# First chunks of the value projection: SP's loads in program order, ScalarE ahead of VectorE on each bank of x, weights cast a pair ahead

## The chip, the cores and the metric

One core of a Trainium2 chip runs the whole kernel. TensorE multiplies, VectorE (DVE) and ScalarE (ACT) do elementwise work, GpSimd (POOL) a little of it, and SyncE (SP) issues nearly all DMAs. The metric is the device time of one execution in microseconds (us); it was 2045.33 us in the median of three runs (2045.03 to 2045.54).

## What is computed

A residual block for 512 tokens of width 2048, in float32: RMSNorm, one projection to queries, keys and values of 16 heads (8 of stick-breaking attention, 8 of forgetting attention) and 8 gates, the two attentions, an output projection, an MLP with squared ReLU, and a last RMSNorm.

```
h = rmsnorm(x, g_attn[l])
proj = jnp.einsum('bsd,de->bse', h, w_in[l])
...
x = x + jnp.einsum('bse,ed->bsd', mixed, w_out[l])
h2 = rmsnorm(x, g_mlp[l])
u = jax.nn.relu(jnp.einsum('bsd,df->bsf', h2, w_up[l]))
x = x + jnp.einsum('bsf,fd->bsd', u * u, w_down[l])
return rmsnorm(x, g_final)
```

The change lies in the first 50 us or so: x is loaded and transposed, and the values of the first two heads and the gates are projected while that goes on.

## The kernel before

**Precision.** A float32 operand is split into a high part (rounded to the type of TensorE's fast float32 mode) and a low part, the operand less its high part. A product is three matmuls: high by high, high by low, low by high (mm3, L75). So for each weight tile ScalarE casts the high part (Piece.cast, L166) and VectorE subtracts it (Piece.low, L170).

**Chunks, pairs, banks.** The 2048 columns of x are 16 chunks of 128. Chunk k and chunk k + 8 are pair k, and the order is 0, 8, 1, 9, ..., 7, 15 (seq, L264). A chunk goes through these steps, each a function of its own:
- turn_x (L230): four TensorE transposes bring 512 tokens of the chunk into one bank of PSUM (tr). The pool has two such banks, so the transposes of a chunk need the bank of the chunk but one before it, read out by everybody.
- x_high (L235): ScalarE scales the bank by g_attn and writes the high part, hH.
- x_low (L238): VectorE reads the bank again, scales it, subtracts hH and writes hL.
- x_more (L241, chunks 0 to 7): ScalarE writes the scaled chunk once more, in two halves, into x1 (x11 and x21).
- x_sum (L244, chunks 8 to 15): VectorE writes f5, the right half of the tokens of this chunk plus x21, and x12, the left half.
- first_values (L259): 12 matmuls, six for each half of the tokens, 128x264 each, into the banks vy and vz.

x1, x12 and f5 are the sources of sums that the later products use (sums_of_x, L330). Reads of one bank by ScalarE and by VectorE are kept apart by semaphores, in the order in which the program issues them.

**Weights.** Chunks 0 and 8 have a piece of weights each, 128x264; pairs 1 to 7 have one of 128x528 for both chunks. Raw pieces (wraw) share three buffers, and each is free again when its low part is formed. The split pieces (wh, wl) have three buffers too.

**The order of the work** is written by hand. Plan.at(t, f) (L148) notes a function with a due time, and Plan.run issues all of them sorted by that time. manual_schedule (L184) keeps TensorE, ScalarE and VectorE in just that order; each of them works strictly in order. SP is not in that list in the kernel before: its DMAs may be put in another order by the scheduler, which works from an estimate of times. Due times count from a notional start: chunk number n in seq is due at 6.5 + 1.93 n (mm_at, L266), and TV (L313) is the end of the last. In the trace SP issued x's first half of columns (xa: chunks 0 to 3 and 8 to 11), pieces 0 and 8 and the weights of pair 1, then xb (chunks 4 to 7 and 12 to 15, two loads of 1024 KB), and then the weights of pairs 2 to 7 mixed with four loads of q.

**What follows.** The values of the next heads come from seven products per group on quadrants of 1024 rows and 384 columns of the weights (product, L390; quadrants q "21", "11", "12", "22", each of four loads of 384 KB by load_quadrant, L304). Quadrant 21 of group 1 has a room of its own. Quadrants 11, 12 and 22 take the room of xa and xb, so their loads (open_quads, L380) wait until x has been squared: square_x (L249), eight ScalarE instructions of 1024 elements that sum the squares of x for its RMSNorm, four on xa and four on xb. The casts of q stand among the squares of xb on ScalarE.

Of the kernel before, what the change touches and what calls it, by code (L numbers as in the profile page):

```python
# [11 lines left out]
ALU = mybir.AluOpType  # L12
PSUM = bass.MemoryType.PSUM

P = 128
# [4 lines left out]
NH = 8  # L20
# [16 lines left out]
def block_kernel(ctx, tc, x, g_attn, w_in, b_f, g_out_sb, g_out_fox, w_out, g_mlp, w_up, w_down, g_final, y):  # L37
    nc = tc.nc
    pe, act, dve, pool, sp = nc.tensor, nc.scalar, nc.vector, nc.gpsimd, nc.sync
# [65 lines left out]
    g_in = cp.tile([P, KC], F32, name="g_in")  # L105
    g_rest = cp.tile([P, KC + 2 * NH], F32, name="g_rest")
    g_up, g_sb, g_fx = g_rest[:, :KC], g_rest[:, KC:KC + NH], g_rest[:, KC + NH:]
    bf = cp.tile([P, NH], F32, name="bf")
# [30 lines left out]
    K8 = KC // 2  # L139
# [43 lines left out]

    manual = tc.manual_schedule(engines={pe.engine, act.engine, dve.engine})  # L184
    manual.__enter__()

    first_piece = q_piece(0, 0, 0)
    with ExitStack() as stage:
# [4 lines left out]
        HALVES = slice(0, 4), slice(4, 8)  # L193

        x1 = vf.tile([P, 2, K8, 2 * P], F32, tag="e0", name="x1")
        x11, x21 = x1[:, 0], x1[:, 1]
# [16 lines left out]
        plan = Plan()  # L213
# [14 lines left out]
        turned = {}  # L228
# [12 lines left out]
        def x_more(k):  # L241
            act.mul(x1[:, :, k, :], turned[k].rearrange("p (s n) -> p s n", s=2), g_in[:, k:k + 1])

        def x_sum(k):  # L244
            g, a = g_in[:, k:k + 1], k - K8
            dve.scalar_tensor_tensor(f5[:, a, :], turned[k][:, 2 * P:], g, x21[:, a, :], op0=ALU.mult, op1=ALU.add)
            dve.tensor_scalar(x12[:, a, :], turned[k][:, :2 * P], g, None, op0=ALU.mult)

# [16 lines left out]
        t0, step = 6.5, 1.93  # L265
        mm_at = {j: t0 + step * n for n, j in enumerate(seq)}  # L266
        LOADS = {0: 1, 1: 1, 2: 2, 4: 4}
        pieces = {}
# [8 lines left out]
        for i, (f, *args) in enumerate(begin):  # L277
            plan.at(-50 + i, f, *args)
        for j in seq:
            k, t = j % K8, mm_at[j]  # L280
            plan.at(t - 2.95 if j else -1.0, turn_x, j)
            plan.at(t - 2.2, x_high, j)
            plan.at(t - 1.45, x_low, j)
            if j < K8:
                plan.at(t - 1.5, x_more, j)
            else:
                plan.at(t - 0.7, x_sum, j)
            w, i = pieces[j]
            if k == 0:
                plan.at(t - 2.1, w.cast)  # L290
                plan.at(t - 1.3, w.low)
            elif j < K8:
                if k > 3:
                    plan.at(t - 13, w.load)
                plan.at(t - 3.2, w.cast)
                plan.at(t - 2.6, w.low)
            for half in range(2):
                plan.at(t + 0.74 * half, first_values, j, w, i, half)
        plan.at(-60, columns, g_in, g_rows, KC)
        for t in range(TB):  # L300
            plan.at(mm_at[4 + t] - 0.8, square_x, 0, t)
        quads = {1: {}, 2: {}}
# [7 lines left out]

        plan.at(mm_at[6], load_quadrant, 1, "21", 0)

# [3 lines left out]
        def load_rows():  # L316
            i = 0
            for r in (g[0].rearrange("(h p) -> h p", p=P) for g in (g_mlp, g_out_sb, g_out_fox)):
                act.dma_start(rows_[i:i + r.shape[0], :], r)
                i += r.shape[0]  # L320
            act.dma_start(bf, b_f.to_broadcast([P, NH]))

# [3 lines left out]

        plan.at(mm_at[3] - 0.8, load_rows)
        plan.at(TV + 0.6, take_rows)
# [4 lines left out]

        plan.at(mm_at[5] - 0.7, sums_of_x, 7, HALVES[0])
        plan.at(mm_at[6] - 0.7, sums_of_x, 6, HALVES[0])
        plan.at(TV + 0.9, sums_of_x, 7, HALVES[1])
# [178 lines left out]
        first_piece.plan(plan, TV + 13 * TP, TV + 14 * TP - 3.5, TV + 14 * TP - 1.5)  # L515
        plan.run()

    acc_cms = [tc.tile_pool(name=f"acc{c}", bufs=2, space=PSUM, reuse_waits="tile") for c in "ab"]
# [1332 lines left out]
```

## Time and profile before

| | |
|---|---|
| median of three runs | 2045.33 us (2045.03 to 2045.54) |
| the profiled execution | 2044.84 us |
| its span in the trace | 2043.1 us |
| HBM read / written | 313.62 MB / 96.49 MB |
| DMA issued through the hardware queues | 408.02 MB, 60.1% of 16 engines' span |

A line of the timeline reads: start in us, duration in us, engine, line of the kernel, operation, output<-inputs, shape, count, and in brackets how long the engine was idle before it and what ended that. PE is TensorE's matmul, PEld its weight load, SPq the issue of DMAs by SP. Consecutive instructions of an engine overlap by some 0.1 us at their ends. A line of the stretches reads: from and to, length, then for each engine its busy time and number of instructions, the clock granted to TensorE, the busy share of the DMA engines, and what they moved. A line of the groups reads: line, engine, operation, tiles and shapes, count, then busy time in all, mean of one in ns, and idle time before them. A line of the chain of waits reads: start, duration, what the end of the kernel hung on at that time. In the trace, hH of chunk n is x_high's output, tr the bank, x without a letter x1 or x12, f is f5.

### The profile page before, as it was taken

The numbers are of one execution on the slowest core, as the hardware profiler recorded it, in microseconds if no ns is written. First come the engines' busy times: TensorE is split into PE (matmuls) and PEld (weight loads), VectorE is DVE, ScalarE is ACT, GpSimd is POOL, SyncE is SP. The second block draws the span as 40 slices with busy tenths as digits, with TensorE's granted clock in tenths as the row PEclk, the third lists the DMA queues.
The fourth block names the chain that finished last, engine by engine and source line by source line (L and its number), as shares of the span: only waits on it lengthen the run. The fifth ranks groups of instructions, "written<-read, shape, count | busy, mean of one in ns | idle before, by whom it ended". The sixth has DMA issues, their size and how long they took to land.

```text
span 2043.1 us, 27164 instructions
## 1 busy us (share of the span) xinstructions
PE 2019.1 (99%) x10410; PEld 1744.4 (85%) x10410; DVE 1735.9 (85%) x1966; ACT 1129.8 (55%) x1618; POOL 64.8 (3%) x73
## 2 busy tenths in 40 slices
PE   8999999999999999999999999999999999999998
PEld 7898888888888888988888888888888888888887
DVE  5975777888867678899999999998798898888896
ACT  6543444455654566667677677676644444444344
POOL 0000011100000000000000000000000000000004
PEclk9999999999999999999999999999999999999999
DMA  5426666665547882656666667667685664674642
GB/s 188 152 94 214 196 206 201 194 218 181 181 134 273 279 277 90 220 173 194 213 193 213 197 197 221 189 206 258 227 293 211 223 253 174 235 249 179 223 163 83
DMA packets 269634, 411.88 MB, mean 202 GB/s; under 512 B 10248, under 2 KB 165432, under 8 KB 262976
## 3 DMA queue, kind: packets, MB, share of 16 engines
q1 hardware_dynamic: 268544, 408.02, 60.1%
q10 hardware_dynamic: 960, 2.13, 0.3%
q8 instruction: 82, 1.34, 0.3%
q14 instruction: 48, 0.39, 0.1%
HBM read 313.62 MB, written 96.49 MB: 201 GB/s over the span
## 4 chain that ended last, share of the span: by engine, by line
PE 92%; DVE 4%; DMA 2%; ACT 1%; issue 1%; SPq 0%; POOL 0%; ACTq 0%; DVEq 0%; POOLq 0%
PE psa L1088 10%; PE accd L78 8%; PE accd L76 8%; PE accd L77 8%; PE accq L76 5%; PE accq L78 5%; PE accq L77 5%; PE psa L1086 5%; PE psc L1088 5%; PE psc L1086 3%; PE psb L1088 3%; PE m L76 1%; PE m L77 1%; PE m L78 1%; PE psb L1086 1%; PE accoa L77 1%
## 5 line engine op out<-in xcount | busy, mean ns | idle before, releaser
L1663 ACT CAST wh<-wd 128x1024 fp32r<-128x1024 f32 x126 | 124.9, 999 | 166.7 <-PE accd L78 57.6
L1553 DVE TENSOR_TENSOR wl<-wu,wh 128x1024 fp32r<-128x1024 f32 x157 | 191.4, 1220 | 15.0 <-ACT wh L1547 14.9
L76 PE MATMUL accq<-hH,wh 128*128 128x512 f32 x512 | 201.7, 394 | 0.0
L78 PE MATMUL accq<-hH,wl 128*128 128x512 f32 x512 | 199.7, 390 | 0.0
L77 PE MATMUL accq<-hL,wh 128*128 128x512 f32 x512 | 199.6, 390 | 0.0
L1547 ACT CAST wh<-wu 128x1024 fp32r<-128x1024 f32 x157 | 166.4, 1060 | 47.5 <-PE psc L1088 20.8
L1088 PE MATMUL psa<-f,wh 128*128 128x512 f32 x728 | 181.1, 391 | 0.0
L77 PE MATMUL accd<-wl,uf 128*128 128x512 f32 x436 | 169.6, 389 | 0.0
L78 PE MATMUL accd<-wh,uf 128*128 128x512 f32 x436 | 169.6, 389 | 0.0
L76 PE MATMUL accd<-wh,uf 128*128 128x512 f32 x436 | 169.4, 389 | 0.0
L1088 PEld LDWEIGHTS psa<-f,wh 128*128 128x128 f32 x728 | 133.7, 188 | 25.8
L1670 DVE TENSOR_TENSOR wl<-wd,wh 128x1024 fp32r<-128x1024 f32 x126 | 144.0, 1152 | 13.2 <-ACT wh L1663 13.2
L1437 DVE TENSOR_TENSOR m<-m,accd 128x1024 f32<-128x1024 f32 x84 | 102.2, 1217 | 47.1 <-PE accd L78 47.1
L1663 ACT CAST wx<-wd 128x1024 fp32r<-128x1024 f32 (+1 forms) x82 | 80.8, 995 | 109.2 <-PE accd L78 43.1
L168 ACT CAST wh<-wraw 128x1024 fp32r<-128x1024 f32 (+2 forms) x77 | 76.7, 998 | 72.6 <-PE accq L77 59.7
L78 PEld LDWEIGHTS accq<-hH,wl 128*128 128x128 f32 x512 | 96.1, 188 | 20.3
L77 PEld LDWEIGHTS accq<-hL,wh 128*128 128x128 f32 x512 | 96.2, 188 | 18.6
L76 PEld LDWEIGHTS accq<-hH,wh 128*128 128x128 f32 x512 | 96.3, 188 | 18.5
L76 PE MATMUL accd<-wx,uf 128*128 128x512 f32 x284 | 110.5, 389 | 0.0
L77 PE MATMUL accd<-wx,uf 128*128 128x512 f32 x284 | 110.5, 389 | 0.0
L78 PE MATMUL accd<-wx,uf 128*128 128x512 f32 x284 | 110.5, 389 | 0.0
L1086 PEld LDWEIGHTS psa<-f,wl 128*128 128x128 f32 x728 | 97.0, 191 | 6.0 <-ACT l L1119 0.6
(418 smaller groups left out, 5110.5 us busy)
## 6 DMA issues: line engine op xcount, KB each, us to landing
wu<-in_w_up_dram SPq DMA_DIRECT2D x60, 1024.0 KB, 6.5
ufd<-st SPq DMA_DIRECT2D x98, 512.0 KB, 3.7
wd<-in_w_down_dram SPq DMA_DIRECT2D x48, 1024.0 KB, 8.4
uf<-ufd SPq DMA_DIRECT2D x42, 1024.0 KB, 6.9
wraw<-in_w_in_dram SPq DMA_DIRECT2D x68, 512.0 KB, 4.2
wo<-wsums SPq DMA_DIRECT2D x28, 512.0 KB, 4.7
q<-in_w_in_dram SPq DMA_DIRECT2D x32, 384.0 KB, 5.4
wd<-in_w_down_dram SPq DMA_DIRECT2D x16, 768.0 KB, 6.1
```

What stands on the lines that cost most here:

```text
L76: pe.matmul(out, sh, mh, start=first, stop=False, skip_group_check=True)
L77: pe.matmul(out, sh, ml, start=False, stop=False, skip_group_check=True)
L78: return pe.matmul(out, sl, mh, start=False, stop=last, skip_group_check=True)
L168: act.copy(self.hi, self.source())
L1086: ins = pe.matmul(ps[:, 2 * P:], lo[:, a, :], f_parts(p, a)[0], start=False, stop=last, skip_group_check=True)
L1088: ins = pe.matmul(ps, hi[:, a, :], f_both(p, a), start=a == PAIRS[0] and p in (1, 5), stop=last, skip_group_check=True)
L1437: dve.tensor_tensor(M[p][:, :, db, :], M[p][:, :, db, :], ps, op=ALU.add)
L1547: act.copy(rooms[k][0], srcs[k])
L1553: lows[0] = dve.tensor_tensor(lo, srcs.pop(k), hi.bitcast(F32), op=ALU.subtract)
L1663: act.copy(rooms[k + 3][0], srcs[k + 3])
L1670: dve.tensor_tensor(rooms[k + 2][1], srcs.pop(k + 2), rooms[k + 2][0].bitcast(F32), op=ALU.subtract)
```

## The change

SP is put under the hand-written order until the value products end (an exit and re-entry of manual_schedule then takes it out again), so DMAs are issued in the order of the plan. x_more moves from ScalarE to VectorE and comes behind x_low there. The half x12 moves from VectorE to ScalarE (x_right, new) and comes ahead of x_low. The due times are rewritten for each pair: on ScalarE x_high of k, the cast for pair k + 1, x_high of k + 8, x_right; on VectorE x_low of k, x_more, the low weights of pair k + 1, x_low of k + 8, x_sum. For the first pair, the transposes of chunk 8 stand between the two halves of chunk 0's matmuls. Squares and sums of x are due later by 1.6 and 2.7, the first quadrant's load is due with chunk 5 rather than chunk 6, and load_rows issues its four small loads from SP.

```diff
@@ -181,7 +181,7 @@
         c0 = (o0 if h >= NH else 0) + h % NH * P + which * WSB
         return Piece(w_in[half * K8 * P:(half + 1) * K8 * P, c0:c0 + P].rearrange("(a p) c -> p a c", p=P), K8, P)
 
-    manual = tc.manual_schedule(engines={pe.engine, act.engine, dve.engine})
+    manual = tc.manual_schedule(engines={pe.engine, act.engine, dve.engine, sp.engine})
     manual.__enter__()
 
     first_piece = q_piece(0, 0, 0)
@@ -239,12 +239,13 @@
             dve.scalar_tensor_tensor(hL[k], turned[k], g_in[:, k:k + 1], hH[k].bitcast(F32), op0=ALU.mult, op1=ALU.subtract)
 
         def x_more(k):
-            act.mul(x1[:, :, k, :], turned[k].rearrange("p (s n) -> p s n", s=2), g_in[:, k:k + 1])
+            dve.tensor_scalar(x1[:, :, k, :], turned[k].rearrange("p (s n) -> p s n", s=2), g_in[:, k:k + 1], None, op0=ALU.mult)
+
+        def x_right(k):
+            act.mul(x12[:, k - K8, :], turned[k][:, :2 * P], g_in[:, k:k + 1])
 
         def x_sum(k):
-            g, a = g_in[:, k:k + 1], k - K8
-            dve.scalar_tensor_tensor(f5[:, a, :], turned[k][:, 2 * P:], g, x21[:, a, :], op0=ALU.mult, op1=ALU.add)
-            dve.tensor_scalar(x12[:, a, :], turned[k][:, :2 * P], g, None, op0=ALU.mult)
+            dve.scalar_tensor_tensor(f5[:, k - K8, :], turned[k][:, 2 * P:], g_in[:, k:k + 1], x21[:, k - K8, :], op0=ALU.mult, op1=ALU.add)
 
         def square_x(half, t):
             x_ = xt[half][:, :, t, :]
@@ -264,7 +265,6 @@
         seq = [j for k in range(K8) for j in (k, k + K8)]
         t0, step = 6.5, 1.93
         mm_at = {j: t0 + step * n for n, j in enumerate(seq)}
-        LOADS = {0: 1, 1: 1, 2: 2, 4: 4}
         pieces = {}
         for j in (0, K8):
             pieces[j] = Piece(w_rows[0][:, j // K8:j // K8 + 1, c0:c0 + m], 1, m), 0
@@ -276,29 +276,28 @@
                  (load_x, 4, 4), (load_x, 12, 4)]
         for i, (f, *args) in enumerate(begin):
             plan.at(-50 + i, f, *args)
-        for j in seq:
-            k, t = j % K8, mm_at[j]
-            plan.at(t - 2.95 if j else -1.0, turn_x, j)
-            plan.at(t - 2.2, x_high, j)
-            plan.at(t - 1.45, x_low, j)
-            if j < K8:
-                plan.at(t - 1.5, x_more, j)
+        for k in range(K8):
+            t, j = mm_at[k], k + K8
+            for jj, dt in ((k, 0.0), (j, step)):
+                for half in range(2):
+                    plan.at(t + dt + 0.74 * half, first_values, jj, *pieces[jj], half)
+            w = pieces[k][0]
+            if k == 0:
+                w8 = pieces[8][0]
+                jobs = [(-5.0, turn_x, k), (-4.0, x_high, k), (-3.9, w.cast), (-3.5, x_low, k), (-3.4, w.low), (-3.3, x_more, k),
+                        (0.1, turn_x, j), (0.2, x_high, j), (0.3, w8.cast), (0.35, x_right, j), (0.4, x_low, j), (0.5, w8.low), (0.6, x_sum, j)]
             else:
-                plan.at(t - 0.7, x_sum, j)
-            w, i = pieces[j]
-            if k == 0:
-                plan.at(t - 2.1, w.cast)
-                plan.at(t - 1.3, w.low)
-            elif j < K8:
+                dt = mm_at[k - 1] - t
+                jobs = [(-2.95, turn_x, k), (-2.2, x_high, k), (-1.5, x_low, k), (-0.75, x_more, k),
+                        (-1.02, turn_x, j), (-0.3, x_high, j), (0.4, x_right, j), (0.85, x_low, j), (1.6, x_sum, j),
+                        (dt + (1.2 if k == 1 else -1.5), w.cast), (dt + (1.3 if k == 1 else -0.05), w.low)]
                 if k > 3:
-                    plan.at(t - 13, w.load)
-                plan.at(t - 3.2, w.cast)
-                plan.at(t - 2.6, w.low)
-            for half in range(2):
-                plan.at(t + 0.74 * half, first_values, j, w, i, half)
+                    jobs.append((-14.0, w.load))
+            for dt, f, *args in jobs:
+                plan.at(t + dt, f, *args)
         plan.at(-60, columns, g_in, g_rows, KC)
         for t in range(TB):
-            plan.at(mm_at[4 + t] - 0.8, square_x, 0, t)
+            plan.at(mm_at[4 + t] + 0.8, square_x, 0, t)
         quads = {1: {}, 2: {}}
 
         def load_quadrant(group, name, i):
@@ -308,7 +307,7 @@
             for a in range(0, K8, 2):
                 sp.dma_start(t_[:, a:a + 2], vrows[s][:, a:a + 2, c0:c0 + NV])
 
-        plan.at(mm_at[6], load_quadrant, 1, "21", 0)
+        plan.at(mm_at[5], load_quadrant, 1, "21", 0)
 
         TV = mm_at[KC - 1] + step - 0.2
         rows_ = xr.tile([KC + 2 * NH, P], F32, name="rows")
@@ -316,23 +315,23 @@
         def load_rows():
             i = 0
             for r in (g[0].rearrange("(h p) -> h p", p=P) for g in (g_mlp, g_out_sb, g_out_fox)):
-                act.dma_start(rows_[i:i + r.shape[0], :], r)
+                sp.dma_start(rows_[i:i + r.shape[0], :], r)
                 i += r.shape[0]
-            act.dma_start(bf, b_f.to_broadcast([P, NH]))
+            sp.dma_start(bf, b_f.to_broadcast([P, NH]))
 
         def take_rows():
             columns(g_rest, rows_, KC + 2 * NH)
             dve.tensor_scalar(g_rest[:, KC:], g_rest[:, KC:], -0.5 / P, None, op0=ALU.mult)
 
-        plan.at(mm_at[3] - 0.8, load_rows)
+        plan.at(mm_at[5] + 0.5, load_rows)
         plan.at(TV + 0.6, take_rows)
 
         def sums_of_x(p, a):
             out, u, v = {7: (x21, x11, x21), 6: (x11, f5, x11)}[p]
             dve.tensor_tensor(out[:, a], u[:, a], v[:, a], op=ALU.subtract)
 
-        plan.at(mm_at[5] - 0.7, sums_of_x, 7, HALVES[0])
-        plan.at(mm_at[6] - 0.7, sums_of_x, 6, HALVES[0])
+        plan.at(mm_at[5] + 2.0, sums_of_x, 7, HALVES[0])
+        plan.at(mm_at[6] + 2.0, sums_of_x, 6, HALVES[0])
         plan.at(TV + 0.9, sums_of_x, 7, HALVES[1])
         for t in range(TB):
             plan.at(TV - 2.4 + (0, 1.8, 3.6, 5.6)[t], square_x, 1, t)
@@ -514,6 +513,10 @@
                 plan.at(t + 7 * TP - 1.0, load_quadrant, 2, "22", 3)
         first_piece.plan(plan, TV + 13 * TP, TV + 14 * TP - 3.5, TV + 14 * TP - 1.5)
         plan.run()
+
+    manual.__exit__(None, None, None)
+    manual = tc.manual_schedule(engines={pe.engine, act.engine, dve.engine})
+    manual.__enter__()
 
     acc_cms = [tc.tile_pool(name=f"acc{c}", bufs=2, space=PSUM, reuse_waits="tile") for c in "ab"]
     accs = [cm.__enter__() for cm in acc_cms]
```

## The prediction

> **What bounds the kernel now.** I read the page first (span, busy shares, chain of waits), then stretches of the first 170 us, then the timeline where TensorE falls behind.
>
> ```profile
> span 2043.1 us, 27164 instructions
> PE 2019.1 (99%) x10410; PEld 1744.4 (85%) x10410; DVE 1735.9 (85%) x1966; ACT 1129.8 (55%) x1618; POOL 64.8 (3%) x73
> PE 92%; DVE 4%; DMA 2%; ACT 1%; issue 1%; SPq 0%; POOL 0%; ACTq 0%; DVEq 0%; POOLq 0%
> ```
>
> TensorE sets the end. All its idle time is 2043.1 - 2019.1 = 24 us, so a change that leaves the matmuls alone, as this one does, can win only from that and from time at a lower clock.
>
> ```profile
> core 0: us, PE busy (x) PEld busy (x) DVE busy (x) ACT busy (x) POOL busy (x), PEclk, DMA share, GB/s
> 7.27:17.64 10.37, 10.35 (x66) 10.09 (x64) 5.01 (x10) 3.58 (x6) 0.00 (x0) 1.00 1.07 396
> 17.64:21.24 3.60, 0.00 (x1) 0.01 (x1) 0.61 (x1) 1.27 (x3) 0.00 (x0) 1.00 1.07 394
> 27.73:47.14 19.41, 19.39 (x155) 18.45 (x154) 15.96 (x27) 16.47 (x29) 0.00 (x0) 1.00 0.14 35
> 60.00:100.00 40.00, 37.98 (x211) 36.06 (x210) 39.45 (x37) 23.69 (x31) 0.00 (x0) 1.00 0.36 126
> 100.00:170.00 70.00, 70.00 (x405) 70.00 (x404) 50.77 (x54) 32.95 (x44) 0.59 (x3) 1.00 0.30 95
> ```
>
> The chunks of x, which end at 47.14, have one hole: 3.60 us without a matmul while the DMA engines are full. The timeline, SP's queue and the chain of waits say what is late:
>
> ```profile
> 17.02 0.60 PE L233 MATMUL tr<-ident,xa 128*128 128x128 f32 x4
> 19.96 0.63 ACT L168 CAST wh<-wraw 128x528 fp32r<-128x528 f32 x1 [5.42 <-DMA wraw<-in_w_in_dram]
> 21.24 0.39 PE L76 MATMUL vy<-wh,hH 128*128 128x264 f32 x1 [3.62 <-ACT hH L236]
> 22.60 0.39 PE L78 MATMUL vy<-wh,hL 128*128 128x264 f32 x1 [0.82 <-DVE hL L239]
> 27.38 0.60 PE L233 MATMUL tr<-ident,xa 128*128 128x128 f32 x4
> 29.28 0.60 PE L233 MATMUL tr<-ident,xb 128*128 128x128 f32 x4
> 31.18 0.60 PE L233 MATMUL tr<-ident,xb 128*128 128x128 f32 x4
> 33.34 0.60 PE L233 MATMUL tr<-ident,xb 128*128 128x128 f32 x4
> ```
>
> ```profile
> 6.22 2.14 SPq L221 DMA_DIRECT2D xb<-in_x_dram  x2
> 8.40 1.88 SPq L309 DMA_DIRECT2D q<-in_w_in_dram  x2
> ```
>
> ```profile
> 10.41 9.46 DMA wraw<-in_w_in_dram
> ```
>
> The weights of pair 2 were issued at 10.41, behind all of xb and two pieces of q, and landed 9.46 us later. ScalarE's cast waited 5.42 us for them with x_high of chunk 2 behind it in ScalarE's order, so TensorE stood 3.62 us, then 0.82 us more for x_low. Where nothing waits, a chunk takes 29.28 - 27.38 = 1.90 us; 33.34 - 31.18 = 2.16 us holds a wait of 0.26 us.
>
> **The change part by part.** Durations first, from the groups by shape between 0 and 47.2 us:
>
> ```profile
> L239 DVE SCALAR_TENSOR_TENSOR hL<-tr,g_in,hH 128x512 fp32r<-128x512 f32 x16 | 11.9, 750 | 13.0 <-ACT x L242 8.0 <-ACT hH L236 4.7
> L236 ACT ACTIVATE hH<-tr,g_in 128x512 fp32r<-128x512 f32 x16 | 11.0, 688 | 12.6 <-PE tr L233 11.7 <-DMA rows<-in_g_out_fox_dram 0.9
> L171 DVE TENSOR_TENSOR wl<-wraw,wh 128x528 fp32r<-128x528 f32 x7 | 4.9, 699 | 4.5 <-ACT wh L168 4.5
> L168 ACT CAST wh<-wraw 128x528 fp32r<-128x528 f32 x7 | 4.4, 635 | 6.1 <-DMA wraw<-in_w_in_dram 6.1
> L251 ACT ACTIVATE xa<-xa 128x1024 f32<-128x1024 f32 x4 | 4.2, 1057 | 0.0
> L247 DVE TENSOR_SCALAR x<-tr,g_in 128x256 f32<-128x256 f32 x8 | 3.8, 474 | 0.0
> L332 DVE TENSOR_TENSOR x<-x 128x1024 f32<-128x1024 f32 x1 | 1.2, 1215 | 0.0
> ```
>
> *The first two chunks.*
>
> ```profile
> 4.80 0.69 ACT L236 ACTIVATE hH<-tr,g_in 128x512 fp32r<-128x512 f32 x1 [2.23 <-PE tr L233]
> 5.39 0.40 ACT L168 CAST wh<-wraw 128x264 fp32r<-128x264 f32 x1
> 5.69 0.69 ACT L242 ACTIVATE x<-tr,g_in 128x512 f32<-128x512 f32 x1
> 6.42 0.75 DVE L239 SCALAR_TENSOR_TENSOR hL<-tr,g_in,hH 128x512 fp32r<-128x512 f32 x1 [2.71 <-ACT x L242]
> 6.54 1.09 PE L233 MATMUL tr<-ident,xa 128*128 128x128 f32 x4 [1.77 <-DMA xa<-in_x_dram]
> 7.08 0.42 DVE L171 TENSOR_TENSOR wl<-wraw,wh 128x264 fp32r<-128x264 f32 x1
> 10.85 0.57 PE L76 MATMUL vy<-wh,hH 128*128 128x264 f32 x1
> 11.22 0.42 PE L77 MATMUL vy<-wl,hH 128*128 128x264 f32 x1
> ```
>
> Before, x_low of chunk 0 started at 6.42, when ScalarE's x_more (5.69 + 0.69) was done, though x_high was done at 5.49. With x_more on VectorE behind it, x_low starts at 5.5 and the low weights are there at 6.6. Chunk 0's matmuls start near 5.9 instead of 7.2, six of them; then chunk 8 is transposed from 7.7, not 6.54, and its x_high ends at 9.5. On ScalarE follow the cast (to 9.8) and x_right (to 10.1); x_low, which reads the same bank and stands behind x_right, runs 10.1 to 10.9, the low weights to 11.2. The second matmul of chunk 8 starts at 11.28; it was 11.22. What chunk 0 wins, chunk 8 gives back: -0.06 us.
>
> *Load queue.* In the plan's order go out: the loads up to chunks 10-11 as before, the weights of pairs 2 and 3, xb, pairs 4 to 7, q. Pair 2 waits for the raw buffer of piece 0 (low part done at 6.6) and then has about 2.6 MB ahead of it (eight chunks of 256 KB, pieces 0, 8 and 1); at the 396 GB/s of the stretch above that ends by 12, and I take 12.6 for the landing, against 19.87. Pair 3 waits for the buffer of piece 8 (11.2), and xb stands behind pair 3 in SP's queue: out from about 11.8 instead of 6.22, its 2.1 MB last 5.3 us, so the halves land near 16 and 19. By the sum below their transposes are due at 22.7 and 24.6: covered, with over 5 us to spare. Pair 4 follows xb and lands near 19.8; its cast stands ahead of chunk 11's x_high, due at 21.1, so some 0.7 us are to spare, the thinnest cover here. q lands by 27 and is cast near 38. load_rows goes from ScalarE's queue to SP's, four small issues behind q whose reader comes after the chunks: nothing waits.
>
> *Pairs 1 and 2.* From chunk 8 on TensorE has the same work in the same order, so the transposes of chunk 10 stay at 17.02. Pair 2's weights are now cast at 12.7 and split by 14.2, x_high of chunk 2 ends at 16.4, x_low at 17.1: its matmuls follow at 17.37, and the transposes of chunk 11 come at 17.02 + 2 x 1.90 = 20.82. They stood at 27.38. **Gain 6.56 us**: the two waits, and the slow clock behind them, which the same view for TensorE alone shows (us, busy, clock, DMA share, GB/s):
>
> ```profile
> 9.13:12.54 3.41, 3.41 (x17) 1.00 1.08 396
> 12.54:15.95 3.41, 3.41 (x30) 1.00 1.05 409
> 22.78:26.19 3.41, 3.41 (x17) 0.52 0.40 89
> ```
>
> At 22.78 to 26.19 the granted clock was 0.52, and 17 matmuls and transposes passed where 30 pass at full speed. The count says that 9.13 to 12.54 ran at half speed too, though its clock column reads 1.00. Each such stretch costs 3.41 / 2 = 1.7 us.
>
> *Pairs 3 to 7.* Per pair VectorE has two x_low, x_more, x_sum and the low weights. x_more as a VectorE tensor_scalar of 512 elements isn't in the trace: at least the 0.47 of 256, at most twice that, 0.95. I take 0.74, because the x_low of the same 512 elements from the same bank takes 0.75. Sum 2 x 0.75 + 0.74 + 0.48 + 0.70 = 3.42 us of the 3.80 that a pair gives; at 0.95 it is 3.63. x_right on ScalarE is at least the 0.40 of the 264-element cast and at most the 0.69 of 512; I take 0.42, by size. ScalarE: 2 x 0.69 + 0.42 + 0.64, and 1.25 with its read-out for the square: 3.7. In time from a chunk's transposes, the square now ends as the next x_high comes due, so the four waits of 0.26 us on x_low (the 2.16) go, 1.0 us. New ones come where the two sums of 1.22 us stand ahead of x_low (0.2 and 0.3 us, 0.1 behind the first), and at chunk 15, where the cast of q (0.84) and x_right now stand between x_high and x_low: 0.5 us. Together 1.1: a net -0.1 us; the bounds on x_more and x_right make it +0.5 to -1.0.
>
> *The products behind.* Order on all engines is that of before, and TensorE and VectorE are both nearly full from 60 to 100 and TensorE wholly to 170, so an earlier start is an earlier end. Late next is what ScalarE still owes: the last square of xa and x_right of chunk 15 now come behind the cast of q, 1.4 us later against the end of the chunks, and quadrant 11's load, which replaces xa, with them:
>
> ```profile
> 44.43 12.42 SPq L309 DMA_DIRECT2D q<-in_w_in_dram  x12
> 56.06 0.82 ACT L168 CAST wh<-q 128x768 fp32r<-128x768 f32 x1
> ```
>
> Twelve loads went out from 44.43, one a microsecond, and the first of them is cast at 56.06: over 7 us of cover, without which the 1.4 us would be lost. At the handover I count 0.1 us for the low part of q's first piece.
>
> Sum: 6.56 - 0.06 - 0.1 - 0.1 = **6.3 us**. The profiled execution took 2044.84 us (span 2043.1 and 1.74 around it), so 2038.5 by it; the median of the runs is 0.49 above it, so **2039.0 us**.
>
> **The rivals.**
>
> *The clock rises a stretch later.* TensorE's new order leaves gaps at 6.1 to 6.6 and 10.9 to 11.28, the second inside the stretch 9.13 to 12.54 after which matmuls became fast. If a stretch must be full, speed comes at 15.95: 1.7 us lost, gain 4.6, 2040.7. For it: 5.72 to 9.13, partly idle, didn't bring the clock up. Against: the gap is 0.4 of 3.41 us. If, on the contrary, the fuller 5.72 to 9.13 suffices, 0.6 us more are won. The Trainium skill (TensorE: Matmul & The Clock Gate, Part 1: The HAM clock gate) calls the window free-running, 3.41 us long, with full speed only after a busy one, so that the point differs from run to run; the steps at 12.54, 22.78 and 26.19 here, three windows and one apart, agree. By that rule the loss could be anything up to 1.7 us in any execution.
>
> *The wait moves to pair 4.* If its load takes the 9.46 us that pair 2's took behind xb, it lands at 13.5 + 9.5 = 23.0, the cast holds up x_high of chunk 11 and TensorE stands 2.4 us, with or without 1.7 of slow clock: gain 3.9 to 2.2, 2041.4 to 2043.1. For it: xb is ahead of it, as it was of pair 2. Against: pair 2 had q ahead of it as well.
>
> *The product stage gives it back.* VectorE is busy 39.45 of 40 us there; if quadrant 11 or VectorE's backlog comes 1.4 us late after all, the gain is 4.9: 2040.4.
>
> *Slower: SP's queue in program order.* One waiting load now holds all behind it. Place: the load of pair 3, which waits for chunk 8's low weights on VectorE, with xb, pairs 4 to 7 and q behind it. Price: each microsecond that it goes out after 11.3 delays pair 4's cast by one beyond the 0.7 of cover, so it takes back the 6.3 us from 18.3 on, and with a second slow stretch from 16.6 on. A load that hangs until 18 would give about 2047. Nothing in the rows makes that buffer so late.
>
> **How the numbers follow.** Forecast 0.52, late clock 0.18, pair 4 0.12, product stage 0.10, slower 0.08. The first, second and fourth are faster by more than 0.2% (4.1 us, about what can be told from no change): 0.80; pair 4 is within it: 0.12; slower 0.08. Range: from 2037.2 (early clock 0.6, x_more at its lower end 0.5, pair of small waits not appearing) to 2042.2, which takes in the late clock, the product stage and half of pair 4.
>
> **What would show it.** Right: no wait of TensorE above 1 us after 12 us, pair 2's weights landed by 13, the last matmul of the chunks near 41, not 47.14, no clock under 1 behind it, SP with xb after pair 3. Wrong: half-speed matmuls after 13, ScalarE waiting for a load at pair 4, x_low waiting at every chunk because x_more takes over 1 us, or a hole between 41 and 60 that isn't there before.

## The result, and the profile after

| | before | after |
|---|---|---|
| median of six runs each | 2045.43 us (2044.83 to 2046.20) | 2038.53 us (2037.76 to 2038.86) |
| ratio of the two, 95% interval | | 0.9966 (0.9953 to 0.9978) |
| the profiled execution | 2044.84 us | 2037.76 us |
| its span | 2043.1 us | 2036.0 us |

The kernel is faster by 0.34%, 6.9 us between the medians, 7.08 us between the two profiled executions; 2039.0 was forecast. (The function open_quads stands at L480 of the kernel before, not where the description above has it.)

The page of the changed kernel, its span and busy times:

```profile
span 2036.0 us, 27169 instructions
PE 2016.1 (99%) x10410; PEld 1741.6 (86%) x10410; DVE 1737.6 (85%) x1966; ACT 1127.9 (55%) x1618; POOL 65.9 (3%) x73
```

TensorE has the same 10410 instructions. Its idle time fell from 24.0 to 2036.0 - 2016.1 = 19.9 us, and its busy time by 3.0 us, most of it time that went at half clock before. Two stretches of the changed kernel, with the bounds and the columns that the forecast used:

```profile
7.27:17.64 10.37, 9.36 (x69) 9.15 (x69) 6.55 (x13) 5.43 (x11) 0.00 (x0) 1.00 0.96 321
17.64:21.24 3.60, 3.60 (x32) 3.58 (x31) 2.93 (x6) 1.74 (x4) 0.00 (x0) 1.00 1.07 397
```

The hole from 17.64 to 21.24, one matmul in 3.60 us before, holds 32 now and is full. A smaller one has come in the stretch ahead of it: 9.36 of 10.37 us. The timeline of TensorE shows where:

```profile
9.46 0.30 PE L76 MATMUL vz<-wh,hH 128*128 128x264 f32 x1
11.59 0.39 PE L77 MATMUL vy<-wl,hH 128*128 128x264 f32 x1 [1.01 <-DVE wl L171]
13.03 0.60 PE L233 MATMUL tr<-ident,xa 128*128 128x128 f32 x4
20.73 0.60 PE L233 MATMUL tr<-ident,xa 128*128 128x128 f32 x4
22.61 0.60 PE L233 MATMUL tr<-ident,xb 128*128 128x128 f32 x4
24.87 0.60 PE L233 MATMUL tr<-ident,xb 128*128 128x128 f32 x4
39.96 0.39 PE L78 MATMUL vy<-wh,hL 128*128 128x264 f32 x1 [0.68 <-DVE hL L239]
41.28 0.34 PE L76 MATMUL vx<-wh,hH 128*128 128x384 f32 x1
43.47 0.24 PE L225 MATMUL trg<-ident,rows 32*128 32x32 f32 x1
```

The transposes of chunk 11 start at 20.73; they stood at 27.38. The first product behind the chunks starts at 41.28 instead of 47.14. Behind 9 us three waits are new: 1.01 us at the second matmul of chunk 8, about 0.4 us between 22.61 and 24.87 (2.26 us where 1.9 would do), 0.68 us at chunk 15. The matmul at 9.46 is the first fast one: 0.30 us, where those before it took 0.42. Speed came about 3 us earlier than before (the matmul at 12.54 there, by the same sign).

ScalarE and VectorE of the changed kernel, at these places:

```profile
9.93 0.48 ACT L245 ACTIVATE x<-tr,g_in 128x256 f32<-128x256 f32 x1
13.10 0.63 ACT L168 CAST wh<-wraw 128x528 fp32r<-128x528 f32 x1 [1.59 <-DMA wraw<-in_w_in_dram]
21.12 0.63 ACT L168 CAST wh<-wraw 128x528 fp32r<-128x528 f32 x1 [1.03 <-DMA wraw<-in_w_in_dram]
6.54 0.74 DVE L242 TENSOR_SCALAR x<-tr,g_in 128x512 f32<-128x512 f32 x1
10.44 0.75 DVE L239 SCALAR_TENSOR_TENSOR hL<-tr,g_in,hH 128x512 fp32r<-128x512 f32 x1 [3.15 <-ACT x L245]
```

ScalarE waits for weights twice: 1.59 us for pair 2's, which harms nobody (x_high of chunk 2 is not due yet), and 1.03 us for pair 4's, with x_high of chunk 11 behind it, which is the step of 2.26 us. VectorE's x_low of chunk 8 starts at 10.44, after x_right (9.93, 0.48 us), and the low weights that TensorE waits for at 11.59 stand behind it. SP's queue and the chain of waits of the changed kernel say how late those were:

```profile
6.66 5.32 SPq L161 DMA_DIRECT2D wraw<-in_w_in_dram  x2
12.02 1.01 SPq L221 DMA_DIRECT2D xb<-in_x_dram  x2
13.14 9.75 SPq L161 DMA_DIRECT2D wraw<-in_w_in_dram  x4
```

```profile
13.14 7.90 DMA wraw<-in_w_in_dram
```

SP keeps the plan's order: the weights of pairs 2 and 3, then xb, then the weights of pairs 4 to 7. The load of pair 4 went out at 13.14 and landed 7.90 us later, at 21.04. The load of pair 3 stood at the head of the queue from 8.0 to 11.60, waiting for its buffer, and nothing went out behind it. By 12 us what had been issued was nearly through, as this stretch shows (the last two columns are the DMA engines' busy share and GB/s):

```profile
12.02:13.14 1.12, 1.12 (x11) 1.12 (x10) 1.12 (x3) 0.04 (x1) 0.00 (x0) 1.00 0.55 84
```

From 13.14 to 15.00 the DMA engines moved 282 GB/s, and only then the 377 to 408 of a full queue.

**What came later.** 6.1 of the 7.08 us were won by the rows' transposition (43.47 against 49.59). Most of the rest comes at two places behind it. At the first transposes of the attention TensorE of the kernel before had a wait; its row, and SP's last store of the value products with the next weight loads:

```profile
176.00 0.74 PE L565 MATMUL trb<-ident,rw 128*128 128x128 f32 x4 [0.55 <-DVE rw L560]
```

```profile
164.77 0.36 SPq L451 DMA_DIRECT2D vd<-s  x1
169.62 1.01 SPq L161 DMA_DIRECT2D wraw<-in_w_in_dram  x2
```

The same of the changed kernel:

```profile
169.18 0.60 PE L568 MATMUL trb<-ident,rw 128*128 128x128 f32 x4
```

```profile
158.66 0.36 SPq L450 DMA_DIRECT2D vd<-s  x1
162.45 1.00 SPq L161 DMA_DIRECT2D wraw<-in_w_in_dram  x2
```

The weights follow the store after 162.45 - 158.66 = 3.79 us instead of 4.85, and the wait of 0.55 us is gone: 176.00 - 169.18 = 6.82 us ahead here. At the start of the MLP the two kernels show, before and after:

```profile
814.35 0.39 PE L78 MATMUL psa<-f,wl 128*128 128x256 f32 x1 [1.03 <-DVE wl L59]
```

```profile
806.88 0.39 PE L78 MATMUL psa<-f,wl 128*128 128x256 f32 x1 [0.30 <-DVE wl L59]
```

The wait fell from 1.03 to 0.30 us; about half of that stays to the end.

### The profile page after: what moved, and what is told of

It is laid out like the page before. It is cut to its first block, busy times and chain, and to the rows that moved or that the text cites. A ratio compares the mean times of both kernels' runs of the same rounds, so it can differ in the third digit from the quotient of the medians.

```text
span 2036.0 us, 27169 instructions
## 1 busy us (share of the span) xinstructions
PE 2016.1 (99%) x10410; PEld 1741.6 (86%) x10410; DVE 1737.6 (85%) x1966; ACT 1127.9 (55%) x1618; POOL 65.9 (3%) x73
## 4 chain that ended last, share of the span: by engine, by line
PE 91%; DVE 5%; DMA 1%; ACT 1%; issue 1%; POOL 0%; SPq 0%; ACTq 0%; DVEq 0%; POOLq 0%
PE psa L1091 10%; PE accd L76 8%; PE accd L77 8%; PE accd L78 8%; PE accq L76 5%; PE accq L78 5%; PE accq L77 5%; PE psa L1089 5%; PE psc L1091 5%; PE psc L1089 3%; PE psb L1091 3%; PE m L76 1%; PE m L77 1%; PE m L78 1%; PE psb L1089 1%; PE accoa L77 1%
```

## The experiments

Each was timed in five rounds beside the kernel before. The place to read them is the rows' transposition, a short piece of TensorE's work 2.2 to 2.5 us behind the start of the first product: 49.59 us before, 43.47 in the changed kernel.

**The changed kernel again.** No edit; it measures what one kernel's profiles differ by.

> The changed kernel once more, to see how far one execution's start differs from another's. Theory: 2037.8 to 2039.0 us, waits as in its first profile, the clock rising somewhere between 9 and 13 us as its window falls. Rival: always at 9.5 us, set by the kernel's own order.

2038.78 us (2038.18 to 2039.06), ratio 0.9967 (0.9954 to 0.9979). Its timeline of TensorE:

```profile
11.75 0.59 PE L77 MATMUL vy<-wl,hH 128*128 128x264 f32 x1 [0.19 <-DVE wl L171]
12.49 0.28 PE L77 MATMUL vy<-wl,hH 128*128 128x264 f32 x1
13.45 0.60 PE L233 MATMUL tr<-ident,xa 128*128 128x128 f32 x4
21.16 0.60 PE L233 MATMUL tr<-ident,xa 128*128 128x128 f32 x4
43.87 0.25 PE L225 MATMUL trg<-ident,rows 32*128 32x32 f32 x1
```

In this execution the matmuls became fast at 12.4, not 9.5, with the same program, and the rows' transposition came 43.87 - 43.47 = 0.4 us later. Of that 0.16 us was there from the first transposes on (3.82 against 3.66), so about 0.25 us is left for the clock. With the slower clock TensorE came to chunk 8's low weights later and waited 0.19 us for them, not 1.01. So the early clock of the first profile was luck, worth some 0.25 us, and comparisons below 0.5 us have to be made at like clock and like start.

**Load order alone.** The kernel before with SP put under the written order, and none of the rest:

```diff
-    manual = tc.manual_schedule(engines={pe.engine, act.engine, dve.engine})
+    manual = tc.manual_schedule(engines={pe.engine, act.engine, dve.engine, sp.engine})
...
         plan.run()
 
+    manual.__exit__(None, None, None)
+    manual = tc.manual_schedule(engines={pe.engine, act.engine, dve.engine})
+    manual.__enter__()
```

> The kernel before, with SP's loads in program order until the end of the value products and nothing else changed: x_more stays on ScalarE ahead of x_low, x12 on VectorE, weights cast just ahead of their own pair. Theory (the load order is the gain: the 3.6 and 0.8 us waits and 1.7 us of slow clock): no wait of TensorE over 1 us between 12 and 28 us, the transposes of chunk 11 at 20.5 to 21.2, 2039.0 to 2039.8 us. Rival (the new order of the readers and the early casts carry a good part): over 2041.5 us, with TensorE waiting for x_low or for the weights in the chunks.

2038.17 us (2037.45 to 2038.77), ratio 0.9963 (0.9949 to 0.9976): faster than the 2039.0 to 2039.8 that was expected. Transposes in its timeline of TensorE:

```profile
17.01 0.60 PE L233 MATMUL tr<-ident,xa 128*128 128x128 f32 x4
19.16 0.60 PE L233 MATMUL tr<-ident,xa 128*128 128x128 f32 x4
21.06 0.60 PE L233 MATMUL tr<-ident,xa 128*128 128x128 f32 x4
23.21 0.60 PE L233 MATMUL tr<-ident,xb 128*128 128x128 f32 x4
43.49 0.24 PE L225 MATMUL trg<-ident,rows 32*128 32x32 f32 x1
```

The hole is closed, and the small waits of the old readers' order are still there: the steps are 2.15, 1.90 and 2.15 us. Its matmuls became fast at 12.7, so its 43.49 is to be held against the 43.87 of the changed kernel's second execution: it is 0.4 us ahead, half of that from the first transposes on (3.64 against 3.82). It has no wait at pair 4. Load order alone carries the whole gain; the other edits add nothing that the times show. The wait at the attention's start is 0.40 us here, so that is one of the things that the load order does not explain.

**All but the load order.** The changed kernel with SP left to the scheduler:

```diff
-    manual = tc.manual_schedule(engines={pe.engine, act.engine, dve.engine, sp.engine})
+    manual = tc.manual_schedule(engines={pe.engine, act.engine, dve.engine})
...
-    manual.__exit__(None, None, None)
-    manual = tc.manual_schedule(engines={pe.engine, act.engine, dve.engine})
-    manual.__enter__()
```

> The changed kernel with SP left to the scheduler again; readers, casts and due times as changed. The order of issue is then xb, weights of pair 2, all of q, weights of pairs 3 to 7. Theory: the holes come back, one at pair 2 (weights landing near 17.8, TensorE idle 1.5 to 2.5 us) and one at pair 3 (landing near 22.4), 2041.5 to 2045 us. Rival: below 2040 us, since the casts a pair ahead take the late weights in their stride.

2050.61 us (2048.97 to 2052.83), ratio 1.0025 (1.0015 to 1.0035): slower than before, and by more than was expected. SP's queue and then TensorE's timeline of this kernel:

```profile
6.74 1.79 SPq L221 DMA_DIRECT2D xb<-in_x_dram  x2
8.65 1.13 SPq L161 DMA_DIRECT2D wraw<-in_w_in_dram  x1
9.82 4.23 SPq L308 DMA_DIRECT2D q<-in_w_in_dram  x4
19.71 9.88 SPq L161 DMA_DIRECT2D wraw<-in_w_in_dram  x5
```

```profile
20.02 0.39 PE L76 MATMUL vy<-wh,hH 128*128 128x264 f32 x1 [4.38 <-ACT hH L236]
50.22 0.24 PE L225 MATMUL trg<-ident,rows 32*128 32x32 f32 x1
817.24 0.58 PE L77 MATMUL psa<-f,wh 128*128 128x256 f32 x1 [3.62 <-DVE f L59]
```

The scheduler put xb ahead of pair 2 again, and four loads of q ahead of the other weights. TensorE's hole is back, 4.38 us against 3.62, and it is 50.22 - 49.59 = 0.6 us behind the kernel before at the end of the chunks. At the attention's start it is level with it (176.01). Some 5 us are lost 800 us later, in a part that the scheduler orders: a wait of 3.62 us, and this stretch at half clock behind it, as its view shows:

```profile
816.00:823.00 7.00, 5.76 (x27) 5.76 (x28) 4.91 (x7) 2.55 (x4) 0.00 (x0) 0.52 0.62 180
```

So the time of this kernel says two things, and only the first is about the chunks. That the rest of the change, without the load order, doesn't close the hole is shown; why the wait at 817 came is open. The kernel before leaves out the same two edits (SP's list, the exit and re-entry) and has no such wait, so the wait takes the rest of the change as well as the scheduler's order; they were not tried apart.

**The old readers' order.** The changed kernel with x_more on ScalarE ahead of x_low, and x12 on VectorE behind x_sum:

```diff
-            dve.tensor_scalar(x1[:, :, k, :], turned[k].rearrange("p (s n) -> p s n", s=2), g_in[:, k:k + 1], None, op0=ALU.mult)
+            act.mul(x1[:, :, k, :], turned[k].rearrange("p (s n) -> p s n", s=2), g_in[:, k:k + 1])
...
-            act.mul(x12[:, k - K8, :], turned[k][:, :2 * P], g_in[:, k:k + 1])
+            dve.tensor_scalar(x12[:, k - K8, :], turned[k][:, :2 * P], g_in[:, k:k + 1], None, op0=ALU.mult)
...
-                jobs = [(-2.95, turn_x, k), (-2.2, x_high, k), (-1.5, x_low, k), (-0.75, x_more, k),
-                        (-1.02, turn_x, j), (-0.3, x_high, j), (0.4, x_right, j), (0.85, x_low, j), (1.6, x_sum, j),
+                jobs = [(-2.95, turn_x, k), (-2.2, x_high, k), (-1.45, x_low, k), (-1.5, x_more, k),
+                        (-1.02, turn_x, j), (-0.3, x_high, j), (0.85, x_low, j), (1.6, x_sum, j), (1.61, x_right, j),
```

> The changed kernel with the readers of each bank as before: x_more on ScalarE ahead of x_low, x12 on VectorE behind x_sum; load order and early casts as changed. Theory: the readers' order is worth little, since it moves waits of 0.2 to 0.7 us from one chunk to the next: 2038.2 to 2039.8 us. Rival (ScalarE first, then VectorE, is what lets the chunks run at 1.9 us): over 2040.5 us, x_low waiting for x_more at each of chunks 0 to 7.

2039.68 us (2039.02 to 2039.92), ratio 0.9971 (0.9959 to 0.9982). In its timeline the rows' transposition stands at 43.35, with matmuls fast from 12.0: 0.5 us ahead of the changed kernel's 43.87 at a like clock. ScalarE comes to pair 4's cast later and waits 0.24 us for its weights instead of 1.0, and from pair 2 on no step between transposes is over 2.17 us. So in the chunks the new order of the readers is worth nothing, and the wait at pair 4 comes with it. What makes the time about 1 us longer is lost later. In the attention it is in this view of TensorE's waits (from 450 to 630 us: in total, times, longest):

```profile
PE accoa L77 <- DMA wl<-wraws: 1.4, 1, 1.4
PE pt L739 <- POOL w L657: 1.1, 1, 1.1
```

The second of them is 0.4 us in the repeated changed kernel and absent in its first profile. At the start of the MLP the wait for wl is 1.0 us here, as in the kernel before, against 0.3 in both executions of the changed kernel. Why GpSimd is late in the attention is open.

**Weights cast just ahead of their pair.**

```diff
-                        (dt + (1.2 if k == 1 else -1.5), w.cast), (dt + (1.3 if k == 1 else -0.05), w.low)]
+                        (-3.2, w.cast), (-2.6, w.low)]
```

> The changed kernel with the weights of pairs 1 to 7 cast and split just ahead of their own pair, as before, instead of a pair ahead. Theory: the cast of pair 4, for which ScalarE waited 1.0 us and TensorE 0.4 us, comes 1.4 us later and waits no more; else nothing: 2037.8 to 2039.0 us. Rival (the early cast hides a wait): over 2039.8 us, TensorE waiting for the weights' low part at some pairs.

2039.31 us (2039.21 to 2039.39), ratio 0.9969 (0.9958 to 0.9981), above the 2037.8 to 2039.0 that was expected and below the rival's 2039.8. The wait for pair 4's load is gone (its steps in the timeline go 20.74, 22.62, 24.60), but x_low falls behind later, with 0.45 us at 33.77, and the rows' transposition comes at 43.80, against 43.47 at the same early clock. By these two executions casting a pair ahead is worth some 0.3 us.

**Transposes of chunk 8 ahead of chunk 0's matmuls**, as they stood before:

```diff
-                        (0.1, turn_x, j), (0.2, x_high, j), ...
+                        (-1.0, turn_x, j), (0.2, x_high, j), ...
```

> The changed kernel with the transposes of chunk 8 ahead of all matmuls of chunk 0, as before. Theory (what chunk 0 wins, chunk 8 gives back): the wait of 1.0 us at chunk 8's second matmul goes, chunk 0 starts 1.3 us later, and the transposes of chunk 11 stay within 0.4 us of the changed kernel's 20.73; 2038.0 to 2039.2 us. Rival (the early matmuls are what brings the clock up at 9.5 instead of 12.7): the clock rises at 12 or later and the transposes of chunk 11 come 1 us later or more, over 2039.5 us.

2038.23 us (2037.96 to 2038.77), ratio 0.9965 (0.9953 to 0.9978). The wait of 1.01 us at chunk 8 is not there, the transposes of chunk 11 come at 20.23, and of this the rows' transposition keeps 43.47 - 42.67 = 0.8 us. By these two executions that is what splitting chunk 0's matmuls costs, although the clock came later here (fast from 10.4, against 9.5); the times of the two kernels do not show it (2038.23 against 2038.53 and 2038.78).

**xb's first half ahead of pair 3's weights.**

```diff
-                 (pieces[1][0].load,), (load_x, 2, 2), (load_x, 10, 2), (pieces[2][0].load,), (pieces[3][0].load,),
-                 (load_x, 4, 4), (load_x, 12, 4)]
+                 (pieces[1][0].load,), (load_x, 2, 2), (load_x, 10, 2), (pieces[2][0].load,), (load_x, 4, 4), (pieces[3][0].load,),
+                 (load_x, 12, 4)]
```

> The changed kernel with only xb's first half ahead of the weights of pair 3 in the load queue. Theory: the DMA engines stay busy while pair 3 waits for its buffer, pair 4's weights land 1.5 to 2.5 us earlier (near 19 instead of 21.1), ScalarE doesn't wait for them, the 0.38 us of TensorE before chunk 4 goes; 2037.6 to 2038.6 us. Rival: pair 3's weights come too late behind xb and TensorE waits at pair 3: over 2039.5 us.

2037.88 us (2037.83 to 2037.93), ratio 0.9963 (0.9951 to 0.9976). The step over pair 4 shrinks from 2.26 to 1.97 us (22.96 to 24.93), and the rows' transposition comes at 43.51, against the 43.87 of the repeated changed kernel at a like clock (both fast from 12.3 to 12.4): 0.36 us, of which 0.08 was there from the first transposes on (3.74 against 3.82). The rest, some 0.3 us, is the wait for pair 4. The same stretch of the DMA engines as above, in this kernel, is full:

```profile
12.02:13.14 1.12, 1.12 (x9) 1.12 (x9) 1.12 (x2) 0.09 (x1) 0.00 (x0) 1.00 1.03 386
```

**All three waits.** The same, with x_right of chunk 8 behind x_low, and the first cast of q behind x_right of chunk 15:

```diff
-                        ... (0.35, x_right, j), (0.4, x_low, j), (0.5, w8.low), (0.6, x_sum, j)]
+                        ... (0.4, x_low, j), (0.42, x_right, j), (0.5, w8.low), (0.6, x_sum, j)]
...
-                        (dt + (1.2 if k == 1 else -1.5), w.cast), ...
+                        (dt + (0.38 if k == 1 else -1.5), w.cast), ...
...
-                    plan.at(t + (-3.3, -1.5, 0.3, 2.3)[n], w.cast)
+                    plan.at(t + (-3.2, -1.5, 0.3, 2.3)[n], w.cast)
```

> The changed kernel with its three remaining waits taken out: xb's first half goes out ahead of the weights of pair 3, chunk 8's x_right comes behind its x_low (with the cast for pair 1 ahead of x_right), and the first cast of q comes behind x_right of chunk 15. Theory: 0.4 (pair 4), 0.5 to 0.7 (chunk 8) and 0.5 (chunk 15) us less until the transposition of the rows after the chunks, at 42.1 to 42.5 instead of 43.47; 2036.6 to 2037.6 us. Rival: the low part of q's second piece, cast later, or the squares of xa, take the place of the waits, and the time stays at 2038 to 2039 us.

2037.64 us (2037.44 to 2038.10), ratio 0.9962 (0.9949 to 0.9976), just above the 2036.6 to 2037.6 that was expected. TensorE's waits up to 170 us in this kernel, and then in the changed one (in total, times, longest); the two that differ are shown, and the second has no row in this kernel:

```profile
PE vy L77 <- DVE wl L171: 0.7, 2, 0.5
```

```profile
PE vy L77 <- DVE wl L171: 1.8, 3, 1.0
...
PE vy L78 <- DVE hL L239: 0.7, 1, 0.7
```

The wait for chunk 8's weights and the one for chunk 15's hL are gone, and the rows' transposition comes at 42.42, with matmuls fast from 11.9. The same kernel once more:

> The changed kernel with the three waits taken out, once more, for its spread: 2037.2 to 2038.1 us, the rows transposed 6.9 to 7.4 us ahead of the kernel before; the rival, that its 0.9 us against the changed kernel was the clock's window or the later stages' chance, has it at 2038.3 us or above.

2038.36 us (2037.56 to 2038.52), ratio 0.9966 (0.9952 to 0.9979): above what was expected, and where the rival had it. The rows' transposition comes at 42.67, 6.92 us ahead of the kernel before, as expected. The clock came early here (fast from 9.6), and still it is 0.25 us behind the other execution of this kernel: TensorE waits 0.33 us for chunk 8's low weights and, at 15.79, 0.64 us for the hL of chunk 9, with ScalarE's cast of pair 2 (for whose weights it waited 1.77 us) ahead of that chunk's x_high. So when TensorE gets there earlier, the landing of pair 2's weights is the next wait. Against the changed kernel's 2038.53 and 2038.78 the two medians are 0.2 to 1.1 us lower: the small waits were real in the trace, but a gain from removing them is no larger than what the runs differ by.

**That and the transposes of chunk 8 first.**

> The changed kernel with the three waits taken out and with the transposes of chunk 8 ahead of chunk 0's matmuls. Theory: both gains add as far as chunk 8's wait isn't counted twice: the transposition of the rows after the chunks near 42.2 (7.2 to 7.6 us ahead of the kernel before), 2036.8 to 2037.8 us. Rival: chunk 0's later start costs what the missing wait at chunk 8 wins: no better than 2037.9 us and the rows' transposition at 42.6 or later.

2039.04 us (2037.59 to 2040.78), ratio 0.9968 (0.9956 to 0.9981). The runs lie 3 us apart; no gain can be told from them, and the median is where the rival had it. In the profiled execution, the fastest of the five, the rows' transposition comes at 41.97, 7.62 us ahead of the kernel before and the earliest of all: about what the theory said, with the clock early (fast from 8.6).

## Why the prediction held, step by step

All in us of lead over the kernel before, from the timelines above, with the repeated execution of the changed kernel beside the first:

| step | forecast | first | again |
|---|---|---|---|
| to the transposes of chunk 9 (13.22 before) | -0.06 | +0.19 | -0.23 |
| from there to those of chunk 11 (27.38 before) | +6.56 | +6.46 | +6.45 |
| to the rows' transposition (49.59 before) | -0.2 | -0.53 | -0.50 |
| to the attention's start (176.00 before) | 0 | +0.70 | +0.69 |
| from there to the end | 0 | +0.3 | -0.6 |

- **The hole of pair 2.** The forecast's main term was right to 0.1 us in both executions: 20.73 - 13.03 = 7.70 and 21.16 - 13.45 = 7.71 us between the transposes, where it stood at 14.16 before. The load order alone gives this gain, and without the load order the hole stays. Pair 2's weights came some 0.5 us later than forecast (13.1, not 12.6), on an engine that had time.
- **The first two chunks.** "What chunk 0 wins, chunk 8 gives back" is what both executions show, within 0.25 us either way. In the working two figures were low: x_right took 0.48 us (0.42 was taken, within its bounds) and x_low started at 10.44, not 10.1, so the second matmul of chunk 8 came at 11.59, not 11.28. In the first execution the early clock covered that. Leaving chunk 8's transposes where they were kept up to 0.8 us where it was tried.
- **Pairs 3 to 7 and the handover.** x_more on VectorE took 0.74 us, as taken. The net of nothing for the readers' order is confirmed: at a like clock the old order, tried both ways, stands at 43.49 and 43.35, and the new one at 43.51 once pair 4's wait is out. What the term lacked is pair 4.
- **Pair 4's cover.** It was called the thinnest, 0.7 us, and it did not hold: landing at 21.04, not 19.8. The forecast had 8.0 us from xb's issue to this landing, with the bytes moving at 396 GB/s from the start; 9.02 went by. They moved at 84 GB/s from 12.02 to 13.14 and at 282 to 15.00: against 396 that is 0.56 MB less, or 1.4 us at that rate, more than the whole miss. The queue had run empty behind pair 3's load. Over these 9.02 us the mean was 331 GB/s, or 2.99 MB; the two loads of xb and the weights of pairs 3 and 4 are at most 2.64 MB of that, and which loads the rest was is open. The rival "the wait moves to pair 4" so happened, at some 0.3 us instead of its 2.4 and more. Sending half of xb ahead of pair 3's weights kept the queue full (386 GB/s) and removed the wait.
- **Chunk 15.** 0.68 us where 0.5 was counted; the cast of q and x_right ahead of x_low are its cause, since changing their order removes it.
- **The clock a stretch later.** It did not happen: the gaps didn't keep the clock down to 15.95 in any run. The second execution had fast matmuls from 12.4, as the forecast took it, and the first from 9.5. That earlier clock, for which 0.6 us had been named, was worth about 0.25, since chunk 8's weights were waited for anyway.
- **The products behind.** "The product stage gives it back" is refuted: the waits there are those of before (1.22, 0.78 and 0.53 us), and the lead grows. What the forecast had at nothing, "an earlier start is an earlier end", brought 0.7 us at the attention's start in both executions. That the wait there went is shown, and that the weights behind the last store came a microsecond sooner; why they did is open. It is not the load order: that alone kept 0.40 us of the wait, with 4.73 us between the store and the weights, while all kernels with the rewritten due times have 3.79 to 4.37 there and no wait, the one without the load order among them (4.20). Nor is it the readers' order, the early casts or the place of chunk 8's transposes, each of which was put back without the wait coming back.
- **The sum.** Forecast 6.3, measured 7.08 and 5.8 us in the two profiled executions and 6.9 in the medians. The steps up to the rows' transposition, all that the forecast gave a figure, brought 6.12 and 5.72. The 0.7 us at the attention's start came in both, and what follows (+0.3 and -0.6) are waits hundreds of microseconds later that change between executions of one kernel. So the mechanism was right, and that the total came within 1 us is in part luck: what was missed at pair 4 and chunk 15 was about made up by the 0.7 us that the forecast had at nothing.
- **Slower by SP's order.** The load of pair 3 did hold the queue, from about 8 to 12 us, and xb left at 12.02 as forecast (11.8). What it cost is pair 4's wait of some 0.3 us, by the empty queue behind it.
- **The signs.** Most of those for a right forecast came: the first product behind the chunks at 41.28, xb behind pair 3, and no new wait above 1 us after 12 us. One of those for a wrong one came too, ScalarE waiting for a load at pair 4 (1.03 us).

## What to carry to other kernels

Where a few loads of different urgency share a queue that a scheduler may reorder, look in the trace at the order in which they were issued before rewriting the compute: here the order of one queue was worth 6 us, and a careful new order of all readers nothing that could be measured. Cover for a load is to be worked out with the rate that the queue will have: here a load that waited at its head let it run empty, and the next 3 us brought 84 and 282 GB/s instead of 396. The thinnest cover is where the next wait stands. A variant that differs in what the scheduler may move can win or lose microseconds far from the edit, so compare the kernels at a landmark right behind the edit as well as at the end.

## What the runs showed of the hardware

The start of fast matmuls lay between 8.6 and 12.7 us over the twelve profiled executions, by where the matmul of 264 columns shortens from 0.42 to 0.28 us, and the same kernel had it at 9.5 and at 12.4. The views of the 3.41 us ahead of that point, and of the 3.41 us behind it, for TensorE alone, first of the changed kernel:

```profile
6.08:9.49 3.41, 3.17 (x14) 1.00 1.07 349
9.49:12.90 3.41, 2.40 (x19) 1.00 0.85 272
```

and the two stretches ahead of the rise in its second execution:

```profile
5.55:8.96 3.41, 2.71 (x11) 1.00 1.06 335
8.96:12.37 3.41, 3.22 (x15) 1.00 0.84 296
```

A stretch that was busy 3.17 or 3.22 of 3.41 us was followed by the fast clock, one busy 2.71 us was not; in the kernel with the three waits taken out and chunk 8's transposes first, 2.81 us from 5.20 to 8.61 were enough; and once up, the clock stayed up through a stretch busy 2.40 us. So a stretch needn't be full, as the first rival supposed. The Trainium skill (TensorE: Matmul & The Clock Gate, Part 1: The HAM clock gate) has a free-running window of about 3.4 us, with a rise after a busy one, and the two executions of one kernel agree with it: what differs between them is where the stretch falls.
